# Hybrid decoder trunk on one core: a separate activation buffer at distance 0 for three uses, earlier transposes of the residual, and a later scaling of the final factors

## The chip, the cores and the metric

The kernel runs as one program on one core of a Trainium2 chip. The metric is the device time of one execution in microseconds; the time before is 628.7 us, the median of three runs (628.1 to 628.72). A profile of a further execution shows where the time of that execution went.

## What is computed

The input is one sequence of 256 tokens with 1024 features in float32. Layer 0 mixes tokens with a gated linear recurrence (8 heads), layer 1 with causal attention (8 heads; with 256 tokens only the own block counts). Each mixer is followed by a SwiGLU feed-forward part with 2816 hidden features, and a last RMSNorm closes the trunk.

```python
h = x
for layer in range(DEPTH):                      # DEPTH = 2
    y = rms_norm(h, norm_mix[layer])
    if layer % N_MIXERS == 0:
        y = hgrn2_mixer(y, hgrn_w_in[idx], hgrn_w_out[idx], lb_all[idx], hgrn_out_norm[idx])
    else:
        y = moba_mixer(y, moba_w_in[idx], moba_w_out[idx], rel_bias_table)
    h = h + y
    g, u = jnp.split(rms_norm(h, norm_ffn[layer]) @ ffn_w13[layer], 2, axis=-1)
    h = h + (silu(g) * u) @ ffn_w2[layer]
return rms_norm(h, final_norm)
```

## The kernel before

**Arithmetic.** Every product of activations with weights is made of three TensorE matmuls in float32r. A weight tile `raw` of 128 x 1024, brought by SyncE's queue, is rounded by ScalarE into `whi` (line 435), and VectorE writes the rest into `wlo` (line 437). An activation is split likewise into a pair with the names `xh`/`xl` (or `hh`/`hl` for the hidden features of the feed-forward parts). `mm_w` issues `whi*xh`, `wlo*xh`, `whi*xl` with the weights as the loaded operand and 256 tokens streaming; `mm_x` (used for the attention's values and for the second feed-forward part's way down) loads 128 tokens of the activation and streams 512 columns of weights. All of them are recorded under one line of the profile, L478 (the helper `mm`), so they are told apart by the names of their tiles and by their place in time.

**Order.** There is no automatic scheduler. The class `Order` holds a planner's clock: the main stream of weight matmuls is issued in the order of the code, and all other work (operations on ScalarE "A", VectorE "V", GpSimd "G", DMA issues "S", and small TensorE work "T") is queued with a due time and issued by `pump` when its inputs are planned to be ready; a "T" operation also waits until it has been ready for `early` ns of planned time (1500 unless it says otherwise). The order on each engine is therefore fixed when the program is built.

**Stages.** The opening and the recurrence's heads (to about 121 us in the trace), its way out (`out_rows` over `us`, to 149 us), feed-forward part 0 (`swiglu`, to 331 us: blocks of 48 matmuls on the way up and 24 on the way down, `down0`), the attention's values, queries and keys (to about 407 us), its way out (`out_rows` over `ao`, to 431 us), feed-forward part 1 (to 618 us: 48 matmuls of 256 tokens on the way up and 12 of 512 columns on the way down, `down1`), the final norm and the output. A part's first four blocks are computed together, over `k`, before the rest run block after block.

**Norms.** `residual` adds a way out to the residual `hT` (lines 632 to 636), splits the new `hT` into the next `xh`/`xl` (565, 567), and squares it (584, 585). `Stats.finish` then folds the sums (606), sums over partitions with two small matmuls (`ones`,`sqacc`), takes the root on GpSimd (617), and spreads it with two transposes (621) whose result ScalarE copies into `rrow` (624).

**Around the end.** The gain of the last norm is read by a DMA on ScalarE's queue into `bt` (1218) and scaled there by ScalarE (1219). `flip_h` transposes `hT` into the token-major `ht` in four groups of four 128 x 128 transposes (1228), each copied out by ScalarE (1231): groups 0 and 1 take the first 128 tokens, groups 2 and 3 the last 128. Only `Final`, at the very end, reads the gain and `ht`.

**Buffers.** `lay_out` places the tiles in a partition's memory. Call distance the start of an activation's buffer less the start of a weight buffer, modulo 256 bytes. Weight buffers take 4096 bytes, activation buffers 1024, and the gap of 48 floats (192 bytes) ahead of the `x` buffers puts all of these at distance 192. The rings `q1` and `k1`, which `hh0` and `hl0` reuse by `alias`, have gaps and widths of their own: their first buffer lies at distance 0, their second one at 192. `hh0`/`hl0` are taken in turn by hidden blocks 0, 7, 14 and 21; with the attention's values taking one turn between, distance 0 falls to blocks 0 and 14 of feed-forward part 0 and to blocks 7 and 21 of part 1. All other activation buffers lie at 192.

Of the kernel before, what the change touches and what calls it, by code (L numbers as in the profile page):

```python
# [15 lines left out]
P = 128  # L16
# [293 lines left out]
def ca(n, ptr=0):  # L310
    return n / 1.2 + 93 + 93 * ptr
# [14 lines left out]
def hybrid_trunk(ctx: ExitStack, tc: tile.TileContext, wts, xT, par, gfin, tab, onehot, masks, out):  # L326
# [10 lines left out]
    def ring(tag, shape, bufs, dt=FT):  # L337
        if tag not in rings:
            rings[tag] = Ring(lambda: sb.tile(shape, dt, name=tag, tag=tag, bufs=bufs), bufs)
        return rings[tag]  # L340
# [4 lines left out]
    def alias(tag, other, shape, dt=FT):  # L345

        o = rings[other]
        wide = [P, S + 48] if other in ("q1", "k1") else shape
        rings[tag] = Ring(lambda: sb.tile(wide, dt, name=tag, tag=other, bufs=o.bufs)[:, :shape[1]], o.bufs)
        rings[tag].past = o.past  # L350

    def lay_out():


        sb.tile([P, 96], FT, name="lead")
        for t in ("whi", "wlo"):
            ring(t, [P, SUB], NSUB, FR).make()
        sb.tile([P, 48], FT, name="gap")
        for k in range(KT):
            for part in "hl":  # L360
                ring(f"x{part}{k}", [P, S], 2, FR).make()
        for part in "qk":

            sb.tile([P, 16], FT, name=f"gap{part}1")
            rings[f"{part}1"] = Ring(lambda part=part: sb.tile([P, S + 48], FT, name=f"{part}1", tag=f"{part}1",
                                                              bufs=2)[:, :S], 2)
            rings[f"{part}1"].make()
            sb.tile([P, 16], FT, name=f"gap{part}2")
        for m in (2, 4, 8, 16, 32, 64):
            for part in "qk":  # L370
                ring(f"{part}{m}", [P, S], 2).make()

    def fixed(tag, shape, dt=FT):
        b = new(tag, shape, 1, dt)
# [6 lines left out]
    def bank(g, held=False):  # L381
        return rings["ps" + g].new(held)
# [97 lines left out]
    class X:  # L480
# [16 lines left out]
        def free(self):  # L497
            for b in (self.h, self.l):
                b.held = False
                b.readers.append(Mark(od.now))  # L500

    def mm_w(o, w, x, start=False, stop=False):
        mm(o, w.hi, x.hi, start=start)
# [299 lines left out]
    class Core:  # L803
# [162 lines left out]
        def result(self):  # L966
            h, so, b4 = self.h, self.so, self.b4
            due = 30
            us[h] = X("x", h)
            hi, lo = us[h].h, us[h].l  # L970
            u = new("u", [P, S], 3)
            od.op("V", 396, lambda: V.scalar_tensor_tensor(u.tile, b4[:, :S], gain(4)[:, h:h + 1], so.tile, op0=OP.mult,
                                                           op1=OP.mult), reads=[b4, so], alloc=[u], due=due)
            sto.add_half(h, lambda: b4[:, :S], [b4], due)
            od.op("A", ca(S), lambda: A.activation(hi.tile, u.tile, AF.Copy), reads=[u], alloc=[hi], due=due)
            od.op("V", cv(S), lambda: V.tensor_tensor(lo.tile, u.tile, hi.tile.bitcast(FT), op=OP.subtract),
                  reads=[u, hi], alloc=[lo], due=due)
# [51 lines left out]
    def swiglu(layer, x, stats, gu, down):  # L1029
# [3 lines left out]
        def hidden(j, b):  # L1033
            gs = new("sgq", [P, S], 3)
            sg = new("u", [P, S], 3)
            due = 6
            od.op("V", cv(S), lambda: V.tensor_tensor(gs.tile, b[:, :S], stats.row.tile, op=OP.mult),  # L1037
                  reads=[b, stats.row], alloc=[gs], due=due)
            od.op("A", ca(S), lambda: A.activation(sg.tile, gs.tile, AF.Sigmoid), reads=[gs], alloc=[sg], due=due)  # L1039
            od.op("V", cv(S), lambda: V.tensor_tensor(gs.tile, gs.tile, sg.tile, op=OP.mult), reads=[sg], writes=[gs], due=due)  # L1040
            od.op("V", cv(S), lambda: V.tensor_tensor(sg.tile, b[:, S:], gs.tile, op=OP.mult), reads=[b, gs], writes=[sg],
                  due=due)
            x = X("h", j % 7)
            hi, lo = x.h, x.l
            od.op("A", ca(S), lambda: A.activation(hi.tile, sg.tile, AF.Copy), reads=[sg], alloc=[hi], due=due + 6)
            od.op("V", cv(S), lambda: V.tensor_tensor(lo.tile, sg.tile, hi.tile.bitcast(FT), op=OP.subtract),
                  reads=[sg, hi], alloc=[lo], due=due + 6)
            hs[j] = x
# [83 lines left out]
    def attend(h, qb, kb):  # L1132
# [59 lines left out]
            mm(b3[:, :S], w[:, :P], pl.tile)  # L1192
            mm(b3[:, P:S], vv[:, 1, hs], pt(slice(0, P)), stop=True)
        od.op("T", ct(P) + 3 * MM, values, reads=[vv, vsplit[h], ptb, ph, pl], alloc=[b3], due=20)
        ao[h] = X("x", h)
        hi, lo = ao[h].h, ao[h].l
        od.op("A", ca(S), lambda: A.activation(hi.tile, b3[:, :S], AF.Copy), reads=[b3], alloc=[hi], due=22)
        od.op("V", cv(S), lambda: V.tensor_tensor(lo.tile, b3[:, :S], hi.tile.bitcast(FT), op=OP.subtract),
# [12 lines left out]
    for k in range(KT):  # L1211
# [4 lines left out]
    gf = new("bt", [P, NH * S])  # L1216
    gf.tile = bt.tile[:, :D]
    od.op("S", 60, lambda: A.dma_start(gf.tile, gfin.to_broadcast([P, D])), writes=[bt], nbytes=524288, due=60)
    od.op("A", ca(D), lambda: A.activation(gf.tile, gf.tile, AF.Copy, scale=-(float(D) ** 0.5) / 2), reads=[bt],
          writes=[gf], due=100)  # L1220
    ht = new("ii", [P, 2, D])

    def flip_h(tt, half):
        b = bank("B")

        def turn():
            for i in range(4):
                T.transpose(b[:, i * P:i * P + P], hT[:, 4 * half + i, tt * P:tt * P + P], ident)  # L1228
        od.op("T", 450, turn, reads=hb, alloc=[b], due=100)
        al = dict(alloc=[ht]) if (tt, half) == (0, 0) else dict(writes=[ht])  # L1230
        o = od.op("A", ca(512), lambda: A.activation(ht[:, tt, 512 * half:512 * half + 512], b[:, :], AF.Copy),
                  reads=[b], due=100 + tt + half, **al)
        if o.alloc == ():
            o.deps.append(ht.writers[0])

# [60 lines left out]
                      reads=[y], nbytes=262144, due=due)  # L1296

    def down1(k, hs, last=False):
        if not acc1:
            acc1[0] = [[main_bank("A") for _ in range(2)] for _ in range(2)]  # L1300
        ks = range(k, FTN if last else k + 1)
        keep["from"] = ws["sub"]
        w = {(kk, nh): piece("ffn_w2", 1, kk, 512 * nh, 512) for kk in ks for nh in range(2)}
        if last:
            od.op("A", 100, lambda: A.activation(warm, ones, AF.Sqrt), due=0)
        for tt in range(2):
            if not last:
                for nh in range(2):
                    mm_x(acc1[0][nh][tt][:, :], hs[k], w[k, nh], tt, start=(k == 0))
                continue  # L1310
            fin = Final(tt)
            for i, (nh, o, n) in enumerate(FIN):
                b = acc1[0][nh][tt]
                for kk in ks:
                    p = w[kk, nh]
                    mm_x(b[:, o:o + n], hs[kk], Piece(p.i, p.c + o, n), tt, stop=(kk == FTN - 1), cost=n / 2.4 + 2.5)
                wrote(b)
                fin.part(i)
            fin.end()
        keep["from"] = None  # L1320
        free_subs(ws["sub"])
        if not last:
            hs[k].free()
# [49 lines left out]
```

## Time and profile before

| | before |
|---|---|
| time, median of 3 runs | 628.7 us (628.1 to 628.72) |
| the profiled execution: time / span | 627.57 us / 625.8 us |
| TensorE clock granted in it | 0.998 |
| VectorE / ScalarE / GpSimd busy | 71% / 58% / 6% |
| DMA, read from HBM | 109.78 MB, 177 GB/s over the span |

The span is the time from the first to the last instruction that the profile holds; the profiled execution's own time is 1.8 us longer, and 1.1 us under the median. A matmul's end is modelled, so its row lasts longer than the step to the next one: the rate is read from the starts, or from the chain that ended last, whose rows give a start, a duration and a count of matmuls that follow each other.

### The profile page before, as it was taken

To read this page: it belongs to the slowest core of one execution; us is meant where nothing else is said; L and a number is where in the kernel's file an instruction comes from. 1 tells how busy PE (TensorE), PEld (TensorE's weight loads), DVE (VectorE), ACT (ScalarE), POOL (GpSimd) and SP (SyncE) were. 2 spreads that over 40 slices of the span, in tenths; PEclk is the share of its full clock that TensorE was granted. 3 is DMA by queue.
4 is the path that set the end of the run, shared out by engine and by line. 5 is a ranking of instruction groups with operands and counts; after the bars stand their busy time and mean duration, and the time that the engine had idled before them with its cause. 6 is when DMAs were issued, how large, how long until landed. Compare 5 with 4: busy or idle time off the path is not lost.

```text
span 625.8 us, 12443 instructions
## 1 busy us (share of the span) xinstructions
PE 615.6 (98%) x4848; PEld 592.8 (95%) x4848; DVE 443.1 (71%) x803; ACT 363.4 (58%) x715; POOL 36.7 (6%) x74
## 2 busy tenths in 40 slices
PE   8999999999999999999999999999999999999995
PEld 7899999999999999999998899999899999999994
DVE  6987989778686666666669678866676666666653
ACT  6779888857554444444447566565664444444443
POOL 0121112100300000000000000000100000000003
PEclk9999999999999999999999999999999999999999
DMA  8962534443996665666653665445645666556501
GB/s 315 331 208 93 179 103 169 132 139 106 236 282 197 201 187 193 195 198 191 189 198 121 215 206 169 139 162 172 202 160 178 203 202 200 184 182 181 163 2 67
DMA packets 31848, 111.83 MB, mean 179 GB/s; under 512 B 3804, under 2 KB 4221, under 8 KB 31789
## 3 DMA queue, kind: packets, MB, share of 16 engines
q1 hardware_dynamic: 30764, 108.71, 53.5%
q0 software_dynamic: 448, 1.25, 1.0%
q10 hardware_dynamic: 576, 1.08, 0.5%
q8 instruction: 38, 0.62, 0.4%
q14 instruction: 22, 0.17, 0.1%
HBM read 109.78 MB, written 1.25 MB: 177 GB/s over the span
## 4 chain that ended last, share of the span: by engine, by line
PE 79%; issue 16%; DVE 3%; DMA 1%; ACT 1%; POOL 1%; SPq 0%; ACTq 0%; DVEq 0%; POOLq 0%
PE psB L478 42%; PE psA L478 36%; DVE wlo L437 1%; DMA raw<-in_w_dram 1%; POOL ny L617 1%; DVE xl L567 0%; DVE yt L632 0%; DVE hT L634 0%; DVE sqacc L585 0%; PE psB L1228 0%; ACT whi L435 0%; PE psA L621 0%; DVE raw L1259 0%; ACT sq L1262 0%; ACT raw L1289 0%
## 5 line engine op out<-in xcount | busy, mean ns | idle before, releaser
L437 DVE TENSOR_TENSOR wlo<-raw,whi 128x1024 fp32r<-128x1024 f32 (+1 forms) x206 | 248.1, 1214 | 110.5 <-ACT whi L435 110.1
L435 ACT ACTIVATE whi<-raw 128x1024 fp32r<-128x1024 f32 (+1 forms) x205 | 213.0, 1050 | 149.0 <-issue 69.9
L478 PE MATMUL psA<-xh,whi 128*128 128x256 f32 x592 | 163.5, 279 | 0.0
L478 PE MATMUL psA<-xh,wlo 128*128 128x256 f32 x592 | 161.8, 277 | 0.0
L478 PE MATMUL psB<-xh,whi 128*128 128x256 f32 x560 | 157.9, 286 | 0.0
L478 PE MATMUL psA<-xl,whi 128*128 128x256 f32 x592 | 157.1, 277 | 0.0
L478 PE MATMUL psB<-xh,wlo 128*128 128x256 f32 x560 | 154.1, 279 | 0.0
L478 PE MATMUL psB<-xl,whi 128*128 128x256 f32 x560 | 149.9, 279 | 0.0
L478 PEld LDWEIGHTS psA<-xh,whi 128*128 128x128 f32 x592 | 111.2, 188 | 0.8 <-issue 0.5
L478 PEld LDWEIGHTS psA<-xh,wlo 128*128 128x128 f32 x592 | 111.3, 188 | 0.3
L478 PEld LDWEIGHTS psA<-xl,whi 128*128 128x128 f32 x592 | 108.2, 188 | 0.0
L478 PEld LDWEIGHTS psB<-xh,wlo 128*128 128x128 f32 x560 | 105.6, 189 | 0.7
L478 PEld LDWEIGHTS psB<-xh,whi 128*128 128x128 f32 x560 | 105.4, 188 | 0.8
L478 PEld LDWEIGHTS psB<-xl,whi 128*128 128x128 f32 x560 | 103.0, 189 | 0.0
L478 PE MATMUL psB<-hl,whi 128*128 128x256 f32 x176 | 48.7, 277 | 0.0
L478 PE MATMUL psB<-hh,whi 128*128 128x256 f32 x176 | 48.7, 277 | 0.0
L478 PE MATMUL psB<-hh,wlo 128*128 128x256 f32 x176 | 48.7, 276 | 0.0
L1039 ACT ACTIVATE u<-sgq 128x256 f32<-128x256 f32 x44 | 18.0, 410 | 38.9 <-DVE sgq L1037 38.7
L478 PE MATMUL psA<-wlo,hh 128*128 128x512 f32 x88 | 34.6, 393 | 0.0
L478 PE MATMUL psA<-whi,hl 128*128 128x512 f32 x88 | 34.5, 392 | 0.0
L478 PE MATMUL psA<-whi,hh 128*128 128x512 f32 x88 | 34.5, 392 | 0.0
L478 PEld LDWEIGHTS psB<-hl,whi 128*128 128x128 f32 x176 | 33.1, 188 | 0.0
(178 smaller groups left out, 789.6 us busy)
## 6 DMA issues: line engine op xcount, KB each, us to landing
raw<-in_w_dram SPq DMA_DIRECT2D x202, 512.0 KB, 4.2
raw<-in_w_dram SPq DMA_DIRECT2D x4, 256.0 KB, 5.0
bt<-scr POOLq DMA_DIRECT2D x8, 128.0 KB, 8.3
hT<-in_x_dram SPq DMA_DIRECT2D x1, 512.0 KB, 6.1
bt<-in_final_dram ACTq DMA_DIRECT2D x1, 512.0 KB, 4.9
out_dram<-raw ACTq DMA_DIRECT2D x2, 256.0 KB, 2.3
out_dram<-raw SPq DMA_DIRECT2D x2, 256.0 KB, 2.0
hT<-in_x_dram SPq DMA_DIRECT2D x2, 128.0 KB, 5.0
```

Source lines behind the costliest of these rows:

```text
L435: od.op("A", ca(n), lambda h=h, r=r, o=o, n=n: A.activation(h[:, :n], r[:, o:o + n], AF.Copy), reads=[r], alloc=[h], due=due)
L437: od.op("V", cv(n), lambda h=h, lo=lo, r=r, o=o, n=n: V.tensor_tensor(lo[:, :n], r[:, o:o + n], h[:, :n].bitcast(FT), op=OP.subtract), rea ...
L478: T.matmul(o, a, b, start=start, stop=stop, skip_group_check=True)
L617: od.op("G", 500, lambda: G.tensor_tensor(y.tile, v.tile, mhalf, op=OP.pow), reads=[v], alloc=[y], due=due)
L1039: od.op("A", ca(S), lambda: A.activation(sg.tile, gs.tile, AF.Sigmoid), reads=[gs], alloc=[sg], due=due)
```

## The change

Three things are edited.

1. `q1` and `k1` become ordinary rings, so all their buffers, and with them `hh0`/`hl0`, lie at distance 192. Behind all rings a gap of 16 floats and one pair `zh`/`zl` is laid out, at distance 0. `across()` hands it out, and it is used for head 0 on the recurrence's way out (`us[0]`), for block 0 of feed-forward part 0, and for head 0 on the attention's way out (`ao[0]`). What is laid out behind the rings moves up by 1088 bytes, 64 bytes modulo 256 and modulo 1024.
2. The transposes of `hT` get a due time of 24 in place of 100, `early` times of 7000, 8500, 10000 and 11500 ns, and PSUM banks of group A in place of B.
3. The scaling of the final gain is issued in `down1` at block 2, in place of ahead of feed-forward part 1.

```diff
-        for part in "qk":
-            sb.tile([P, 16], FT, name=f"gap{part}1")
-            rings[f"{part}1"] = Ring(lambda part=part: sb.tile([P, S + 48], FT, name=f"{part}1", tag=f"{part}1",
-                                                              bufs=2)[:, :S], 2)
-            rings[f"{part}1"].make()
-            sb.tile([P, 16], FT, name=f"gap{part}2")
-        for m in (2, 4, 8, 16, 32, 64):
+        for m in (1, 2, 4, 8, 16, 32, 64):
             for part in "qk":
                 ring(f"{part}{m}", [P, S], 2).make()
+        sb.tile([P, 16], FT, name="gap2")
+        for part in "hl":
+            ring(f"z{part}", [P, S], 1, FR).make()
...
+    def across():
+        return X("z", "", 1)
...
-            us[h] = X("x", h)
+            us[h] = X("x", h) if h else across()
...
-            x = X("h", j % 7)
+            x = across() if (layer, j) == (0, 0) else X("h", j % 7)
...
-        ao[h] = X("x", h)
+        ao[h] = X("x", h) if h else across()
...
-    od.op("A", ca(D), lambda: A.activation(gf.tile, gf.tile, AF.Copy, scale=-(float(D) ** 0.5) / 2), reads=[bt],
-          writes=[gf], due=100)
...
-        b = bank("B")
+        b = bank("A")
...
-        od.op("T", 450, turn, reads=hb, alloc=[b], due=100)
+        od.op("T", 450, turn, reads=hb, alloc=[b], due=24, early=7000.0 + 1500.0 * (2 * tt + half))
...
     def down1(k, hs, last=False):
+        if k == 2:
+            od.op("A", ca(D), lambda: A.activation(gf.tile, gf.tile, AF.Copy, scale=-(float(D) ** 0.5) / 2), reads=[bt],
+                  writes=[gf])
```

How the order moves is seen at three places; the number in a name is that of the buffer in the built program, and the lines of the changed kernel are 473 for 478, 430 for 435 and 1226 for 1228.

TensorE, in the first four blocks of feed-forward part 1, at the spread of the norm's factor (`ident,ny`), before:

```order
L478 MATMUL psB<-xh_6022,whi 128x256
L478 MATMUL psB<-xh_6022,wlo 128x256
L478 MATMUL psB<-xl_6041,whi 128x256 x4
L621 MATMUL psA<-ident,ny 128x128 x2
L478 MATMUL psB<-xl_6041,whi 128x256 x4
L478 MATMUL psB<-xh_6069,whi 128x256
```

And after:

```order
L473 MATMUL psB<-xh_6021,wlo 128x256
L473 MATMUL psB<-xl_6040,whi 128x256 x2
L1226 MATMUL psA<-ident,hT 128x128 x4
L621 MATMUL psA<-ident,ny 128x128 x2
L473 MATMUL psB<-xl_6040,whi 128x256 x6
L473 MATMUL psB<-xh_6067,whi 128x256
L473 MATMUL psB<-xh_6067,wlo 128x256
L1226 MATMUL psA<-ident,hT 128x128 x4
```

The first group of transposes stands right ahead of the spread, the second eight matmuls behind it, the third ten matmuls on.

TensorE, at the first block on the way down in feed-forward part 1, where two of the four groups stood before:

```order
L478 MATMUL psB<-xl_6041,whi 128x256
L1228 MATMUL psB<-ident,hT 128x128 x4
L478 MATMUL psB<-xh_6069,whi 128x256
L478 MATMUL psB<-xh_6069,wlo 128x256
L478 MATMUL psB<-xl_6079,whi 128x256
L1228 MATMUL psB<-ident,hT 128x128 x4
```

After, none is left there; the fourth group stands earlier, behind the first step of the fifth block on the way up:

```order
L473 MATMUL psB<-xh_5989,wlo 128x256
L473 MATMUL psB<-xl_6009,whi 128x256
L1226 MATMUL psA<-ident,hT 128x128 x4
L473 MATMUL psB<-xh_5999,whi 128x256
L473 MATMUL psB<-xh_5999,wlo 128x256
```

So all four groups come before the first block on the way down, where two stood inside it or behind it.

ScalarE, around the last norm ahead of feed-forward part 1, before:

```order
L565 ACTIVATE xh_6022<-hT,pv 128x256
L1218 DMA bt<-in_final_dram 128x1024
L584 ACTIVATE sq<-hT 128x512
L1219 ACTIVATE bt<-bt 128x1024
L565 ACTIVATE xh_6069<-hT,pv 128x256
L565 ACTIVATE xh_6071<-hT,pv 128x256
```

And after:

```order
L565 ACTIVATE xh_6021<-hT,pv 128x256
L1218 DMA bt<-in_final_dram 128x1024
L584 ACTIVATE sq<-hT 128x512
L565 ACTIVATE xh_6067<-hT,pv 128x256
L565 ACTIVATE xh_6069<-hT,pv 128x256
```

The scaling of the gain is no longer between the squares of the first half of `hT` and the splits of the second half; it stands some 30 rows later, among the blocks of feed-forward part 1.

More of the change, by code (lines that the diff above doesn't have):

```diff
@@ L347, in alias @@
         o = rings[other]
-        wide = [P, S + 48] if other in ("q1", "k1") else shape
-        rings[tag] = Ring(lambda: sb.tile(wide, dt, name=tag, tag=other, bufs=o.bufs)[:, :shape[1]], o.bufs)
+        rings[tag] = Ring(lambda: sb.tile(shape, dt, name=tag, tag=other, bufs=o.bufs), o.bufs)
         rings[tag].past = o.past
@@ L1228, in turn @@
                 T.transpose(b[:, i * P:i * P + P], hT[:, 4 * half + i, tt * P:tt * P + P], ident)
-        od.op("T", 450, turn, reads=hb, alloc=[b], due=100)
+        od.op("T", 450, turn, reads=hb, alloc=[b], due=24, early=7000.0 + 1500.0 * (2 * tt + half))
         al = dict(alloc=[ht]) if (tt, half) == (0, 0) else dict(writes=[ht])
         o = od.op("A", ca(512), lambda: A.activation(ht[:, tt, 512 * half:512 * half + 512], b[:, :], AF.Copy),
-                  reads=[b], due=100 + tt + half, **al)
+                  reads=[b], due=24 + tt + half, **al)
         if o.alloc == ():
```

## The prediction

> **What bounds the kernel now.** I read the page first: busy times, then the chain that ended last.
>
> ```profile
> PE 615.6 (98%) x4848; PEld 592.8 (95%) x4848; DVE 443.1 (71%) x803; ACT 363.4 (58%) x715; POOL 36.7 (6%) x74
> ...
> PE 79%; issue 16%; DVE 3%; DMA 1%; ACT 1%; POOL 1%; SPq 0%; ACTq 0%; DVEq 0%; POOLq 0%
> ```
>
> TensorE is the bound nearly everywhere, so only two things can move the time: how fast its matmuls follow each other, and where it stands still. The chain, in order of time, shows the first (start, duration, what, count):
>
> ```profile
> 164.89 0.22 PE psB L621 x2
> 165.11 13.39 PE psA L478 x118
> 178.50 2.86 PE psB L478 x24
> ...
> 186.82 2.72 PE psB L478 x24
> ...
> 292.90 2.86 PE psB L478 x24
> ...
> 515.16 5.47 PE psB L478 x48
> 520.62 2.73 PE psA L478 x12
> 523.36 5.65 PE psB L478 x48
> 529.01 2.77 PE psA L478 x12
> ...
> 599.14 5.65 PE psB L478 x48
> ```
>
> Matmuls of 256 tokens come at two rates. The good one is 2.72/24 = 113.3 ns a step. The bad one is 5.65/48 = 117.7 ns; it begins at 523.4 and is still there at 599.1. It begins right behind the block at 520.62, which is hidden block 7 of feed-forward part 1, one of the four that use the buffer at distance 0; the other two in sight, at 178.50 and 292.90, are blocks 0 and 14 of part 0, where each step takes 2.86/24 = 119.2 ns. There the good rate follows. So distance 0 costs some 6 ns a step where the activation streams, and where it is the loaded operand (part 1) a lasting bad rate follows. Is it the clock? The two stretches side by side (engines' busy time, then clock, DMA share, GB/s):
>
> ```profile
> 466.30:515.00 48.70, 48.70 (x358) 45.75 (x357) 31.12 (x42) 22.70 (x31) 0.00 (x0) 1.00 0.60 189
> 523.40:604.60 81.20, 81.20 (x588) 76.58 (x587) 51.16 (x66) 36.63 (x48) 0.00 (x0) 1.00 0.51 159
> ```
>
> The granted clock is 1.00 in both and DMA is lighter in the slow one, so it is neither. The rate is a state of TensorE's stream which, once taken, lasts until something breaks the stream.
>
> Where TensorE stands still, its timeline at the norm ahead of feed-forward part 1 shows (start, duration, last the idle time and what ended it):
>
> ```profile
> 438.71 0.62 PE L478 MATMUL psB<-xl,whi 128*128 128x256 f32 x4
> 440.14 0.58 PE L478 MATMUL psA<-ones,sqacc 128*128 128x1 f32 x4 [0.81 <-DVE sqacc L606]
> ...
> 443.01 0.63 PE L478 MATMUL psB<-xl,whi 128*128 128x256 f32 x4
> 444.07 0.43 PE L621 MATMUL psA<-ident,ny 128*128 128x128 f32 x2 [0.42 <-POOL ny L617]
> ```
>
> Four steps from 438.71 end at 439.16, and the sums start at 440.14: 0.98 us lost. Four slow steps from 443.01 end at 443.48, and the spread starts at 444.07: 0.59 us lost.
>
> **Part 1 of the change: the gain's scaling moves.** Who is late at 440.14? The other engines' timelines (idle time last):
>
> ```profile
> 433.36 1.28 DVE L636 TENSOR_TENSOR hT<-psA,hT 128x512 f32<-128x512 f32 x2
> 435.03 1.06 ACT L1219 ACTIVATE bt<-bt 128x1024 f32<-128x1024 f32 x1 [2.39 <-DMA bt<-in_final_dram]
> 436.00 0.89 ACT L565 ACTIVATE xh<-hT,pv 128x256 fp32r<-128x256 f32 x2
> 436.52 0.89 DVE L567 SCALAR_TENSOR_TENSOR xl<-hT,pv,xh 128x256 fp32r<-128x256 f32 x2 [1.88 <-ACT xh L565]
> 439.57 0.42 DVE L606 TENSOR_TENSOR sqacc<-sqacc 128x256 f32<-128x256 f32 x1
> 439.91 2.36 DVE L437 TENSOR_TENSOR wlo<-raw,whi 128x1024 fp32r<-128x1024 f32 x2
> 442.18 0.15 DVE L614 TENSOR_SCALAR nv<-psA 128x2 f32<-128x2 f32 x1
> 442.41 1.60 POOL L617 TENSOR_TENSOR ny<-nv,mhalf 128x2 f32<-128x2 f32 x1 [97.87 <-DVE nv L614]
> ```
>
> The second half's `hT` begins to be there at 434.04 (433.36 + 0.68), but ScalarE sits behind the scaling, which waits 2.39 us for its DMA, and splits only at 436.00; VectorE stands 1.88 us for it. With the scaling gone this chain starts 1.88 us sooner, the limit being `hT` itself. The folded sums end at 439.99 - 1.88 = 438.11, ahead of 439.16: **-0.98**. Next late: `nv` on VectorE, behind two weight remainders of 2.36 us, at about 440.5, and the root, 1.60 us, ends near 442.2. TensorE reaches the spread at 443.48 - 0.98 = 442.50, and after the change the first four transposes stand ahead of it as well: **-0.59**, with some 0.3 us to spare even without these. The scaling (1.06 us) goes to block 2, where ScalarE is busy 22.70 of 48.70 us; the wait for the DMA is long over. At nothing; without that cover it would cost its 1.06 us.
>
> **Part 2: the transposes move.** Their number is the same. In the place that they leave, and at the spreads, the chain reads:
>
> ```profile
> 142.32 0.22 PE psA L621 x2
> 142.54 6.71 PE psB L478 x57
> ...
> 460.73 0.44 PE psB L1228 x4
> 461.17 1.06 PE psB L478 x9
> ...
> 465.79 0.44 PE psB L1228 x4
> 466.23 5.12 PE psB L478 x45
> ```
>
> A group takes 0.44 us and brings one longer step behind it, before as after: 0, with bounds of 0.15 us to either side for rates in the short stretches between. Their copies go ahead on ScalarE (a group of 0.60 us each, below) of the factor's copy and of weight roundings:
>
> ```profile
> 444.54 0.39 ACT L624 ACTIVATE rrow<-psA 128x256 f32<-128x256 f32 x1 [2.96 <-PE psA L621]
> L1231 ACT ACTIVATE ii<-psB 128x512 f32<-128x512 f32 x4 | 2.4, 599 | 1.6 <-PE psB L1228 1.6
> ```
>
> ScalarE stood idle for 2.96 us just there, so 2.4 us fit. But each group also breaks the stream, and these rows show that the rate behind a break is either: 6.71/57 = 117.7 and 1.06/9 = 117.8 against 5.12/45 = 113.8 and, behind the spread at 164.89, 13.39/118 = 113.5. Of the groups in this excerpt, the one at 460.73 reads the first 128 tokens and leaves the bad rate, the last one reads the other 128 and leaves the good one. The two differ by 512 bytes in where `hT` lies against the stream's buffer, 160 and 672 bytes modulo 1024; after the change it is 96 and 608. The last group is again of the second kind, and I take it to leave the good rate. This decides much, since behind it no break comes until the end.
>
> **Part 3: the buffers.** Block 7 of part 1 is no longer at distance 0, so nothing turns the rate at 520. The blocks at 515.16 and 523.36 differ by 0.18, the ways down behind them by 0.04 at most; ten of the one (523.36 to 599.14 at 8.42 us a round) and nine of the other: 1.8 + 9 x 0.02 = **-2.0**. Block 14 of part 0 falls from 2.86 to 2.72: **-0.14**. Block 0 was at distance 0 and stays so. `ao[0]` newly pays **+0.14**. `us[0]` pays between 0 and 0.14, as its stretch is cut up by the heads' own matmuls and partly slow already: **+0.1**.
>
> The tiles behind the rings move by 64 bytes, so breaks ahead of 178 us may fall the other way. Known ones: the spread at 164.89 now leaves 118 steps at 113.5; at 117.7 they would cost 0.5, until the block at distance 0 behind it. Others, like 57 steps behind 142.54, could win 0.25. Bounds -0.5 to +0.8; I take **+0.3**, by the spread at 142.32: its factor's tile lies 448 bytes modulo 1024 from the stream's buffer, as that at 164.89 will (512 now), and it leaves the bad rate.
>
> **Sum.** -0.98 - 0.59 - 2.0 - 0.14 + 0.14 + 0.1 + 0.3 = -3.2 us, against the profiled execution's 627.6: 624.4. The median of the runs shown is 1.1 us above that execution, so the forecast is 628.7 - 3.2 = **625.5 us**.
>
> [...]
>
> **Rivals.**
> *The last group of transposes leaves the bad rate.* For: two of the four stretches quoted behind a break are slow, 608 has no row. Against: the row at 465.79. Price: the 2.0 isn't won, and the 67 us up to 523, now good, turn bad (the fourth group stands some 30 steps ahead of the place that the first one leaves at 459.9, so at about 456) at 0.2 us a round of 8.2: +1.6. 628.7 - 3.2 + 2.0 + 1.6 = 629.1.
> *Feed-forward part 0 stays slow* (slower than before). If the spread at 164.89 leaves the bad rate, and block 0 at distance 0, entered from the bad rate, doesn't restore the good one, 150 us from 181 to 331 run at 117.7: 72 steps a round of 8.16 us, 18.4 rounds, 4.4 ns each: +5.8. Both must happen. For: the spread at 142.32. Against: both rows at distance 0 are followed by the good rate; yet both are entered from it. 625.5 + 0.2 (the rest of the 0.5) + 5.8 = 631.5.
> *The stalls don't close*, the sums being held by something that the scaling hides: 625.5 + 1.6 = 627.1. Against: VectorE's row with 1.88 names ScalarE alone.
> *The buffer does nothing*: the rate at 523 turns for another reason, by the time in the stream, and turns again: 625.5 + 2.0 = 627.5. Against: rounds at 515.16 and before are alike, and it turns in the very block at distance 0.
>
> **How the numbers follow.** Chances: forecast 0.62, last group 0.16, part 0 slow 0.07, stalls stay 0.09, buffer without effect 0.06. The forecast's own spread, from the bounds of parts 2 and 3 (-0.8 and +0.5 about the value taken, 0.15 for the transposes, 0.1 for `us[0]`) and 0.1 for the measurement, is 624.3 to 626.4. The range reaches up to the last group's 629.1, and leaves out part 0 and the tails: 624.3 to 629.3. 0.2% is 1.26 us, about what a measurement of this kernel can tell from no change, so faster is below 627.4: nearly all of 0.62, 0.07 of the stalls' case and 0.03 of the buffer's, less tails: 0.71. Slower, over 630.0: 0.08. Between: 0.21.
>
> **What would show it.** In the profile after: the sums and the spread in feed-forward part 1 without idle time ahead of them; ScalarE's splits within 0.2 us of `hT`; rounds of 8.2 us from the last transposes to the end; block 14 of part 0 at 2.72; `ao[0]`'s 24 steps near 119 ns. A round of 8.4 us behind the fourth group would prove me wrong on the rate, steps of 117.7 between 181 and 331 would show the dear case, and idle time at the sums that names another engine the third.

## The result and the profile after

The changed kernel takes 623.98 us, the median of four runs (623.45 to 624.26), against 628.4 us for the kernel before on the same chip (627.93 to 628.72): a ratio of 0.9933 [0.992, 0.9947]. The direction of the forecast was right. Its size was not: 623.98 lies 1.5 us under the 625.5 us forecast and 0.3 us under the low end of the range. The profiled execution took 623.94 us, with a span of 622.2 us. One execution of the kernel before, of 682.65 us at a granted clock of 0.849, is left out of every comparison below.

The page of the changed kernel, first TensorE's busy time and share, then the shares of the chain that ended last:

```profile
PE 613.2 (99%) x4848; PEld 591.3 (95%) x4848; DVE 443.0 (71%) x803; ACT 363.6 (58%) x715; POOL 36.7 (6%) x74
...
PE 96%; DMA 2%; DVE 1%; ACT 1%; issue 0%; SPq 0%; ACTq 0%; DVEq 0%
```

Before, 79% of the chain lay on TensorE and 16% was put down to "issue", since the chain left TensorE at the spread and followed GpSimd's empty queue backwards. Now nearly all of it lies on TensorE, and it no longer leaves TensorE at the spread.

The chain of the changed kernel in order of time (start, duration, what, count), at the places that the prediction spoke of:

```profile
143.04 6.49 PE psB L473 x57
...
165.09 13.40 PE psA L473 x118
178.49 2.86 PE psB L473 x24
...
292.89 2.72 PE psB L473 x24
...
446.07 9.88 PE psB L473 x87
455.95 0.44 PE psA L1226 x4
456.39 5.13 PE psB L473 x45
...
519.02 2.75 PE psA L473 x12
521.76 5.47 PE psB L473 x48
...
595.68 5.47 PE psB L473 x48
```

From the last group of transposes at 455.95 to the end, every block takes 5.47 us; the bad 5.65 us of before is gone, and block 7 (519.02) takes 2.75 us as its neighbours do. Block 14 of feed-forward part 0 (292.89) takes 2.72 us for 2.86. The 118 steps behind the spread at 164.87, for which I feared the bad rate, take 13.40/118 = 113.6 ns; the 57 steps at 143.04, slow before, take 6.49/57 = 113.9.

The other engines' timelines at the norm ahead of feed-forward part 1 (start, duration, engine, line, operation, and last the idle time with what ended it):

```profile
433.49 1.28 DVE L636 TENSOR_TENSOR hT<-psA,hT 128x512 f32<-128x512 f32 x2
434.21 0.91 ACT L565 ACTIVATE xh<-hT,pv 128x256 fp32r<-128x256 f32 x2 [1.44 <-DVE hT L636]
437.80 0.43 DVE L606 TENSOR_TENSOR sqacc<-sqacc 128x256 f32<-128x256 f32 x1
439.30 0.50 PE L473 MATMUL psA<-ones,sqacc 128*128 128x1 f32 x4
440.41 0.15 DVE L614 TENSOR_SCALAR nv<-psA 128x2 f32<-128x2 f32 x1
440.64 1.60 POOL L617 TENSOR_TENSOR ny<-nv,mhalf 128x2 f32<-128x2 f32 x1 [96.28 <-DVE nv L614]
442.25 0.60 PE L1226 MATMUL psA<-ident,hT 128*128 128x128 f32 x4
442.68 0.38 PE L621 MATMUL psA<-ident,ny 128*128 128x128 f32 x2
```

ScalarE splits at 434.21, right behind the first of the two additions (433.49 + 0.68 = 434.17, one addition taking 0.68 us), and its wait now names `hT`. The folded sums end at 438.23, ahead of TensorE's 439.30; the root ends at 442.24, and TensorE passes through the first group of transposes to the spread at 442.68. No idle time stands in either of TensorE's rows.

Stage by stage, each worked out from the start of the first weight matmul of a stage to that of the next stage's first, in the two profiled executions (times of the profile before):

| stage | before | after | difference | forecast |
|---|---|---|---|---|
| opening, from 5.0 us to 22.8 | 17.86 | 18.20 | +0.34 | 0 |
| recurrence's heads, to 121.5 | 98.65 | 98.89 | +0.24 | with the next row |
| way out of the recurrence and part 0's first four blocks, to 178.3 | 56.85 | 56.28 | -0.57 | +0.4 |
| part 0 from block 0, to 331.0 | 152.64 | 152.48 | -0.16 | -0.14 |
| attention's heads and its way out, to 431.5 | 100.48 | 100.78 | +0.30 | +0.14 |
| part 1's norm, transposes and first way down, to 469.8 | 38.37 | 36.63 | -1.74 | -1.57 |
| part 1, to 523.2 | 53.37 | 53.39 | +0.01 | 0 |
| part 1, behind block 7, and the tail | 102.59 | 100.56 | -2.03 | -2.0 |

The sum is -3.61 us, and the two profiled executions differ by 627.57 - 623.94 = 3.63 us. By medians the gain is larger, 628.4 - 623.98 = 4.4 us. Two things were to be explained: the terms that differ from the forecast, and the difference between medians and profiles.

### The profile page after: what moved, and what is told of

Same layout as the page of the kernel before. It is cut to its first block, busy times and chain, and to the rows that moved or that the text cites. A ratio compares the mean times of both kernels' runs of the same rounds, so it can differ in the third digit from the quotient of the medians.

```text
span 622.2 us, 12444 instructions
## 1 busy us (share of the span) xinstructions
PE 613.2 (99%) x4848; PEld 591.3 (95%) x4848; DVE 443.0 (71%) x803; ACT 363.6 (58%) x715; POOL 36.7 (6%) x74
## 4 chain that ended last, share of the span: by engine, by line
PE 96%; DMA 2%; DVE 1%; ACT 1%; issue 0%; SPq 0%; ACTq 0%; DVEq 0%
PE psA L473 50%; PE psB L473 45%; DMA hT<-in_x_dram 1%; DMA raw<-in_w_dram 1%; PE psB L1180 0%; PE psA L1226 0%; DVE wlo L432 0%; ACT sq L584 0%; ACT xh L565 0%; PE psA L621 0%; DVE raw L1257 0%; ACT sq L1260 0%; ACT raw L1287 0%; DVE sqacc L585 0%; PE psB L621 0%
## 5 line engine op out<-in xcount | busy, mean ns | idle before, releaser
L473 PE MATMUL psA<-xh,whi 128*128 128x256 f32 x584 | 161.0, 279 | 0.0
L473 PE MATMUL psA<-xh,wlo 128*128 128x256 f32 x584 | 159.5, 276 | 0.0
L473 PE MATMUL psA<-xl,whi 128*128 128x256 f32 x584 | 154.9, 277 | 0.0
L473 PE MATMUL psB<-xh,whi 128*128 128x256 f32 x552 | 154.7, 284 | 0.0
L473 PE MATMUL psB<-xh,wlo 128*128 128x256 f32 x552 | 151.2, 278 | 0.0
L473 PE MATMUL psB<-xl,whi 128*128 128x256 f32 x552 | 146.9, 278 | 0.0
L473 PE MATMUL psB<-hl,whi 128*128 128x256 f32 x168 | 46.4, 276 | 0.0
L473 PE MATMUL psB<-hh,whi 128*128 128x256 f32 x168 | 46.4, 276 | 0.0
L473 PE MATMUL psB<-hh,wlo 128*128 128x256 f32 x168 | 46.4, 276 | 0.0
L473 PEld LDWEIGHTS psB<-hh,whi 128*128 128x128 f32 x168 | 31.5, 188 | 0.0
```

The source lines that it names most:

```text
L473: T.matmul(o, a, b, start=start, stop=stop, skip_group_check=True)
```

## The experiments

Twelve more runs were made, each with a profile: one of the kernel before, two of the changed kernel, and nine of eight variants. The first took the kernel before once more, unchanged, to see what the 1.1 us between its median and its profiled execution are.

> The kernel before, unchanged, profiled a second time. Open is why its first profiled execution (627.57 us) lies 0.8 us under the median of its runs, while that of the changed kernel lies on its median. Theory: other executions of it run some stretch at the other of the two rates of matmuls (113.3 or 117.7 ns a step), so this profile, if it comes out near 628.4 us, shows some 0.8 us more in one named stretch, about 180 steps at the bad rate. Rival: the excess is spread evenly or lies outside the span; then all stretches agree with the first profile within 0.1 us and only the span or what is around it grows.

Measured: 628.37 us (627.9 to 630.27, ten executions); every stage behind the opening agrees with the first profile within 0.02 us, except the stage with the stall at the sums, 9.21 for 9.12 us. The opening takes 18.66 for 17.86 us. So this execution, at the median, has no stretch at the other rate: it has a longer opening and a slightly longer stall. That doesn't explain the median, though: over all 14 traces of this document the opening takes 17.28 to 18.66 us, so that the first profile's 17.86 is an ordinary one and this 18.66 the longest. The theory of a stretch at another rate doesn't hold for this execution; that others have none isn't shown, and the run with the transposes alone, below, has one.

**One part alone: the scaling of the gain** (the transposes and the buffers as before).

```diff
-    od.op("A", ca(D), lambda: A.activation(gf.tile, gf.tile, AF.Copy, ...), reads=[bt], writes=[gf], due=100)
...
     def down1(k, hs, last=False):
+        if k == 2:
+            od.op("A", ca(D), lambda: A.activation(gf.tile, gf.tile, AF.Copy, ...), reads=[bt], writes=[gf])
```

> Only the scaling of the final gain is moved; buffers and transposes are those of before. Theory: both stalls at the norm ahead of feed-forward part 1 go, 0.98 + 0.59 us, and nothing else changes: 1.6 us off the span, between the way out of the attention and the first block on the way down; the bad rate from 523 us on stays. Rival: without the transposes ahead of the spread the second stall stays in part: between 1.0 and 1.6 us.

Measured: 626.62 us (626.26 to 626.9, seven executions), a ratio of 0.997 [0.9959, 0.9981]. Its chain at the two places:

```profile
435.99 3.64 PE psB L478 x32
439.62 0.34 PE psA L478 x4
439.96 2.94 PE psB L478 x24
442.89 0.22 PE psA L621 x2
443.11 16.02 PE psB L478 x136
```

The sums (439.62) and the spread (442.89) follow the matmuls ahead of them without a gap: both stalls are gone, without any transposes ahead of the spread. But the 136 steps behind the spread take 16.02 us, where the kernel before has 15.44: behind the break stands the bad rate now, and it takes back 0.58 us. Summed over the norm and the first way down, the profile's gain is 1.1 us, and by the medians it is 1.7. The executions lie within 0.64 us of each other; those of the kernel before lie between 627.25 and 630.27 us over all chips. That the wait on the gain's DMA makes the difference in spread is likely, and not shown: the ten executions with the transposes alone, which wait for it as well, lie within 1.15 us.

**One part alone: the buffers** (the first edit of the change, its part of the diff above down to `ao[h]`; scaling and transposes as before).

> Only the buffers are changed (the rings q1 and k1 plain, the separate pair at distance 0 for three uses); the scaling and the transposes are those of before. Theory: the bad rate behind block 7 of feed-forward part 1 doesn't begin, 2.0 us; block 14 of part 0 wins 0.16; the first head of the attention's way out costs 0.3; the heads of the recurrence, whose tiles have moved, come out within 0.5 us of before: 1.9 us off the span in sum. Rival: the last group of transposes, which in this order stands behind the first block on the way down, leaves the bad rate, and the rounds stay at 8.4 us: 0 to 1.6 us longer than before.

Measured: 629.49 us (626.17 to 631.2, ten executions), a ratio of 1.0001 [0.998, 1.0021]. The buffers alone win nothing in the median. The chain, from the wait on the gain to block 7:

```profile
429.26 5.57 DMA bt<-in_final_dram
...
440.54 4.46 PE psB L473 x24
...
466.53 0.44 PE psB L1228 x4
466.97 5.30 PE psB L473 x45
...
517.14 5.65 PE psB L473 x48
```

Two things are to be seen. The last group of transposes, at 466.53, here leaves the bad rate (5.30/45 = 117.8 ns, where before had 113.8), and it lasts from there on (5.65 us for 48 steps at 517.14, 4.48 us for 38 at 525.56), through blocks that have nothing at distance 0: this is the first rival of the prediction, and it took back what the buffer won. And 24 steps at 440.54 take 4.46 us, 186 ns each. The windows of this kernel, the stretch from 440.90 and one behind it, say what that is (from and to, the stretch, the busy times, then granted clock, DMA share, GB/s); the last row is the same place in the kernel before:

```profile
440.90:444.30 3.40, 3.40 (x19) 3.40 (x19) 2.38 (x4) 0.50 (x1) 1.60 (x1) 0.53 0.62 182
445.00:449.00 4.00, 4.00 (x37) 4.00 (x36) 2.36 (x2) 2.83 (x4) 0.00 (x0) 1.00 0.54 197
...
440.50:444.00 3.50, 3.15 (x26) 2.94 (x26) 2.97 (x4) 1.07 (x2) 1.59 (x1) 1.00 0.58 160
```

And its timeline, ScalarE's wait and TensorE's (idle time last):

```profile
434.86 1.06 ACT L1219 ACTIVATE bt<-bt 128x1024 f32<-128x1024 f32 x1 [3.07 <-DMA bt<-in_final_dram]
439.96 0.58 PE L473 MATMUL psA<-ones,sqacc 128*128 128x1 f32 x4 [1.48 <-DVE sqacc L606]
```

Here ScalarE waited 3.07 us for the gain (2.39 before), TensorE stood idle for 1.48 us (0.81 in the same row of before), and just behind that its granted clock fell to 0.53 for 3.4 us. The stage in which that lies took 12.84 us for 11.94: another 0.9 us, although the stall at the spread is gone there. The ten executions lie in two clumps, four between 626.17 and 626.5 us and six from 629.44 on; the profile belongs to the upper one. The lower clump is 2 us under the kernel before's 628.35 us on that chip, what the forecast gave this part. No profile of it exists, so whether the good rate, the clock or both make it stays open.

**Block 7 back at distance 0**, all else as after.

```diff
-            x = across() if (layer, j) == (0, 0) else X("h", j % 7)
+            x = across() if (layer, j) in ((0, 0), (1, 7)) else X("h", j % 7)
```

> The changed kernel, with the separate pair at distance 0 used a fourth time, for hidden block 7 of feed-forward part 1. Theory: that block, the loaded operand at distance 0, turns the rate from 113.3 to 117.7 ns a step, and it stays so to the end: rounds of 8.4 in place of 8.2 us from about 521 us on, 2.0 us longer than the changed kernel, nothing else changed. Rival: the rate of before turned at that place for another reason (the time in the stream, or the double rings); then the rounds stay at 8.2 us and the time is that of the changed kernel within 0.1 us.

Measured: 625.71 us (625.4 to 626.17), a ratio of 0.9959 [0.9944, 0.9974]. Its chain:

```profile
513.73 5.47 PE psB L473 x48
519.20 2.73 PE psA L473 x12
521.93 5.65 PE psB L473 x48
...
597.71 5.66 PE psB L473 x48
```

The rate turns in block 7 and stays bad to the end: the 612 weight matmuls from there on take 86.95 us for 84.88. That is +2.07 us for the -2.0 of the prediction, and every other stage behind the opening is as after.

**After once more, the halves swapped, and block 0 and the two others at 192.** These three ran on one chip. In the second, groups 0 and 1 take the last 128 tokens and groups 2 and 3 the first:

```diff
+        s = 1 - tt
...
-                T.transpose(b[:, i * P:i * P + P], hT[:, 4 * half + i, tt * P:tt * P + P], ident)
+                T.transpose(b[:, i * P:i * P + P], hT[:, 4 * half + i, s * P:s * P + P], ident)
...
-        o = od.op("A", ca(512), lambda: A.activation(ht[:, tt, 512 * half:512 * half + 512], b[:, :], AF.Copy),
+        o = od.op("A", ca(512), lambda: A.activation(ht[:, s, 512 * half:512 * half + 512], b[:, :], AF.Copy),
```

> The changed kernel, unchanged, profiled a second time. Theory: it has left few breaks behind which the rate can fall either way, so its executions agree: span within 0.4 us of 622.2, and every stretch within 0.1 us of the first profile. Rival: its rates differ from execution to execution, and one stretch differs by 0.3 us or more.

Measured: 623.57 us (623.25 to 624.23), a ratio of 0.9923 [0.9907, 0.9939]; each stage as in the first profile within 0.04 us, except the opening, 17.77 for 18.20 us.

> The changed kernel with the two halves of the tokens swapped in the groups of transposes: groups 0 and 1 take the last 128 tokens, groups 2 and 3 the first, so that the group behind which no break comes any more reads the 512 bytes that the prediction takes to leave the bad rate. Theory (where hT lies against the stream's buffer, modulo 1024 bytes, decides: 96 bad, 608 good): the rounds behind the fourth group, from about 456 us on, are 8.4 in place of 8.2 us to the end, 3.7 us longer than the changed kernel. Rival: the rate behind a break is set by something else; the rounds stay at 8.2 us and the time is that of the changed kernel.

Measured: 623.82 us (623.44 to 624.46), a ratio of 0.9927 [0.9911, 0.9942]. Its chain behind the third and the fourth group:

```profile
445.60 9.88 PE psB L473 x87
...
455.91 5.13 PE psB L473 x45
```

The same 9.88 and 5.13 us as after, although the address that each group reads against the stream's buffer is that of the other half. So the bytes modulo 1024, by which the prediction chose the good rate for the last group, do not decide it, for these two breaks.

For the third, the gap ahead of the separate pair grows by 192 bytes, so that it lies at distance 192, and what follows stays where it is after the change:

```diff
-        sb.tile([P, 16], FT, name="gap2")
+        sb.tile([P, 64], FT, name="gap2")
...
+        sb.tile([P, 208], FT, name="fill")
```

> The changed kernel with the separate pair at distance 192 in place of 0; a filler keeps all other addresses modulo 1024 bytes. Theory: distance 0 costs where it is used and restores nothing here, since all the stretches ahead of it are at the good rate already: block 0 of feed-forward part 0 wins 0.16, the attention's first head 0.3, the recurrence's first head 0 to 0.2: 0.5 to 0.7 us shorter than the changed kernel. Rival: distance 0 is what leaves the good rate behind it; then the stretch behind one of the three uses runs at 117.7 ns a step, up to 5.8 us longer in feed-forward part 0.

Measured: 623.36 us (623.03 to 623.42), a ratio of 0.9917 [0.9899, 0.9935]. Its chain at block 0 of part 0 and at the last group of transposes:

```profile
178.09 2.72 PE psB L474 x24
...
455.60 5.30 PE psB L474 x45
```

Block 0 takes 2.72 for 2.86 us, and the `ao` matmuls 10.66 for 10.83. The last group leaves the bad rate here (5.30 us for 45 steps), yet it holds only to the first block on the way down: from 463.7 on the good one stands. With the buffers alone it had passed through the blocks on the way down (2.77 us each at 514.37 and 522.79, and still 5.65 us for 48 steps between them). Part 0 runs at the good rate with nothing at distance 0 ahead of it, so block 0 restores nothing there. The profiled span, 621.6 us for 622.2 after, fits both: by an estimate from 5.65 and 5.47 us a block, the bad rate in the 17 blocks behind 463.7 would have added 3.1 us, and in part 0 some 5.8 us by the prediction's estimate. Whether distance 0 would restore the good rate from the bad one was not put to the test, since no run entered block 0 at the bad rate.

**The tiles behind the rings back at their old place modulo 1024** (960 bytes more ahead of them), all else as after:

```diff
+        sb.tile([P, 240], FT, name="fill")
```

> The changed kernel with a filler of 960 bytes behind the separate pair, so that what is laid out behind the rings (identity, hT, the factors, the masks, the attention's tiles) lies as before modulo 1024 bytes. Theory: the 64 bytes by which these had moved set the rates behind the breaks of the recurrence; so the 57 steps behind the spread at 142 us, good after the change, are bad again (+0.25 us), and those to 153 us with them (+0.15), while the heads from 56 to 62 us and 103 to 121 us go back as well; the groups of transposes leave the same rates as after the change. In sum within 0.5 us of the changed kernel. Rival: the rates of the recurrence were set by q1 and k1 at distance 192 or by us[0] at 0, and stay as after the change.

Measured: 623.71 us (623.41 to 624.06), a ratio of 0.9924 [0.9908, 0.994]. Its chain at the spreads:

```profile
142.16 6.71 PE psB L474 x57
...
164.72 13.39 PE psA L474 x118
```

The 57 steps are at 6.71 us again, as before the change. The twelve runs and the two first profiles give 14 traces: in the six with the old addresses these 57 steps take 6.71 or 6.72 us, in the eight with the new ones 6.49. So the 64 bytes do set this stretch. From the 240th to the 672nd weight matmul, among the recurrence's heads, 75.25 us pass here and 75.51 after; the next two stages, to 149 and to 167 us, take 27.55 and 18.36 us here, 27.32 and 18.08 after. So the move by 64 bytes is worth +0.26 - 0.23 - 0.28 = -0.25 us, where the prediction had +0.3. And `us[0]` at distance 0, which this kernel has and the kernel before has not, costs nothing: 27.55 for 27.61 us.

**The wait made longer.** The kernel before, with a second read of the gain into a part of `bt` that nothing uses then, ahead of the gain's own:

```diff
+    od.op("S", 60, lambda: A.dma_start(bt.tile[:, D:], gfin.to_broadcast([P, D])), writes=[bt], due=59.9)
```

> Before with a second read of the gain (512 KB more, into a half of a buffer that nothing uses then) ahead of the gain's own DMA, so that the scaling and with it the sums wait longer; TensorE's order is that of before. Theory (TensorE waits for the scaling, and a longer wait also halves the clock for some 3.4 us, as in the run with the buffers alone): the stall at the sums grows by about 1 us or more from 0.98 us, behind it some 16 steps take about 214 ns, 3120-3188 takes 10 us or more for 9.12 us, 3188-3284 about 12.8 us for 11.94 us, and the median lies 1.5 to 3 us above before. Rival (only the wait counts, the clock was chance): the steps behind it stay at 113 to 120 ns, and the median rises by the wait alone. Second rival (the gain doesn't set the wait): 3120-3188 stays within 0.1 us of 9.12 us.

Measured: 632.08 us (630.79 to 633.72, four executions, of which the profiled one was the longest), a ratio of 1.0056 [1.0037, 1.0075]. Two pieces of its chain:

```profile
430.69 7.93 DMA bt<-in_final_dram
...
444.72 5.21 PE psB L478 x24
```

Its windows, from the end of the wait to behind the spread:

```profile
443.70:447.20 3.50, 3.46 (x16) 3.49 (x17) 3.37 (x4) 1.47 (x2) 1.19 (x1) 0.50 0.39 129
447.20:449.90 2.70, 2.70 (x16) 2.70 (x15) 0.00 (x0) 0.00 (x0) 0.41 (x1) 0.55 0.89 267
450.00:454.00 4.00, 4.00 (x37) 4.00 (x36) 2.36 (x2) 2.79 (x4) 0.00 (x0) 1.00 0.29 109
```

And its timeline at the sums (idle time last):

```profile
443.74 0.98 PE L478 MATMUL psA<-ones,sqacc 128*128 128x1 f32 x4 [4.20 <-DVE sqacc L606]
```

TensorE stands still for 4.20 us, and the clock is 0.50 to 0.55 for the next 6.2 us: 24 steps in 5.21 us, 217 ns each. That is nearly twice as long as in the run with the buffers alone, and more steps than the 16 that I expected. The stage with the stall takes 12.91 us (9.12 before), the next 13.89 (11.94). Both parts of the theory came out, TensorE's wait for the scaling and about half the clock behind it, and the price of the longer wait was more than expected: 3.8 us more in the stage with the wait (its idle time grew by 3.39) and 1.95 us more in the next in this execution, the longest of the four; the median rose by 3.7. The clock fell inside the stall here: from 438.60 to 443.70 it is 0.91.

**One part alone: the transposes** (scaling and buffers as before):

```diff
-        b = bank("B")
+        b = bank("A")
...
-        od.op("T", 450, turn, reads=hb, alloc=[b], due=100)
+        od.op("T", 450, turn, reads=hb, alloc=[b], due=24, early=7000.0 + 1500.0 * (2 * tt + half))
...
-                  reads=[b], due=100 + tt + half, **al)
+                  reads=[b], due=24 + tt + half, **al)
```

The due time of ScalarE's copies moves with that of the transposes, here as in the whole change.

> Before with the placing of the residual transposes alone changed: they go out in blocks 0 to 3 of part 1's way up, and the gain is scaled where before scales it and the buffers stay. Theory (sum of parts): the stall at the sums stays (3120-3188 about 9.1 us for 9.12 us), the stall at the spread (0.59 us) is kept or filled in part by the first group, the bad rate behind block 7 is gone if a group now ends it (523 to the end 84.9 us for 86.94 us): median about 626.0 us, 2.0 to 2.6 us under before. Rival (the transposes need the other two edits to be free): a group waits for a bank or for the scaling, 3188-3408 longer than 29.3 us, and the median lies within 1 us of before.

Measured: 628.25 us (627.8 to 628.95, ten executions), a ratio of 0.9996 [0.9986, 1.0005]: no difference. Its chain:

```profile
443.31 1.61 POOL ny L617
...
515.81 5.47 PE psB L478 x48
521.28 2.73 PE psA L478 x12
524.01 5.66 PE psB L478 x48
```

My expectation was wrong where it gave the -2.0 to this part. The groups end at 458, some sixty us ahead of block 7, and no break comes behind block 7; so it turns the rate as before (5.47 at 515.81, 5.66 at 524.01). The way out of the first block gains 1.84 us, the stages ahead of it lose 0.22, 1.14 and 0.46: the 1.76 us of transposes are carried from one place to another, nothing more. The root still comes late, and TensorE still waits for it at the spread.

One more thing is to be seen in it: up to 440 us TensorE's order and all addresses are those of the kernel before, yet behind the three small transposes at 415.68 the steps run at 117.8 ns here, and at 113.3 ns in both profiles of the kernel before. The attention's last small matmuls, at 419.19, hand the bad rate on to the 105 steps behind them, and it lasts to the stall; from 414.31 to 432.13 it costs 0.57 us. The rate behind that break isn't settled by order and addresses alone.

**The version without distance 0 against the changed kernel**, both once more, on one chip.

> The changed kernel with the separate buffer at distance 192 in place of 0, a second time, beside the changed kernel itself on the same chip. Theory (distance 0 costs time where its three uses stand and its rate is given back by none of them): 672 to 864 about 27.1 us for 27.3 us, block 0 of part 0 2.72 us for 2.86 us, the ao matmuls 10.66 us for 10.83 us, the fourth group's leaving 10.43 us for 10.25 us; median 0.2 to 0.5 us under the changed kernel's in the same job. Rival (the opening decides): the medians lie within 0.15 us.

> The changed kernel unchanged, on the same chip as the version without distance 0. Theory: 623.25 to 624.3 us as in its earlier runs, every stage behind the opening within 0.05 us of the first profile, and 0.2 to 0.5 us above the version without distance 0. Rival: the opening's spread (17.3 to 18.7 us) covers that difference, and the medians lie within 0.15 us.

Measured: 623.25 us (622.9 to 623.57, five executions) without distance 0, 623.71 us (623.32 to 624.32, six) for the changed kernel; ratios to before 0.9914 [0.9901, 0.9926] and 0.9923 [0.991, 0.9935]. The medians differ by 0.46 us, as expected; the stages account for less. Block 0 (-0.14), the `ao` matmuls (-0.17) and the last group's leaving (+0.18) come out as the first time, but the stage with `us[0]` takes 27.32 us, as after, and not 27.11: in the first profile 57 steps between 129 and 136 us had the good rate, in this one they have not. The last 24 of them, in the first profile and in this one:

```profile
133.45 2.74 PE psB L474 x24
...
133.22 2.83 PE psB L474 x24
```

The two profiles are of one and the same kernel, so order and addresses don't settle the rate here either. Behind the opening the two profiles of this job differ by 0.2 us. So the version without distance 0 has the lowest medians of all that ran, by 0.21 us under the changed kernel on the first chip and 0.46 on the second, with intervals that overlap; less than half of the 0.46 is in a stage that I could name.

## Why the prediction was wrong in size, and right in direction

**The bound and the two rates.** Right. That distance 0 turns the rate in block 7, and that the turn lasts to the end, is shown from both sides: the 612 weight matmuls from there on take 2.06 us less after the change, and 2.07 us more with block 7 put back and all else equal. The rival by which the buffer does nothing has fallen. That a rate lasts until something breaks the stream was said too firmly: without distance 0 the bad rate (5.30 us for 45 steps) ended at the first block on the way down, at 463.7, behind which no group of transposes stands.

**The stalls.** Right: -1.74 for -1.57, the order of waits was as forecast (the fold 438.23 for 438.11, the root 442.24 for 442.2), and the run with the scaling alone shows that the scaling's place, and not the transposes, closes both.

**The transposes.** Right at 0 when alone. But that the last group leaves the good rate was a guess on a wrong reason: the halves swapped leave the same rates. It came true in the changed kernel and in its repeats; in the run with the buffers alone, with the group at its old place, it did not, and the bad rate from there on took back the 2 us in the profiled execution; without distance 0 the group left the bad rate too, for 45 steps. That it left the good one here was luck, and what decides it stays open. The chance of 0.16 for that rival was no overestimate.

**Block 14 and `ao[0]`.** -0.14 forecast, 2.72 for 2.86 measured; +0.14 forecast, +0.17 by the run without distance 0. Of this only some 0.1 is in the steps of `ao[0]`, at 120 ns; the rest is in the 18 steps of the next head, which run at 118 ns behind it, so distance 0 under the streaming operand wasn't always followed by the good rate. With the tiles back at their old place these 18 are at 113 ns again. Part 0 didn't turn slow, and block 0 had no part in that.

**First step that failed: "+0.3" for the 64 bytes and "+0.1" for `us[0]`.** In the two rows of the table between 22.8 and 178.3 us they came to +0.24 - 0.57 = -0.33 us instead of +0.4. The run with the tiles back puts the 64 bytes at -0.25 and `us[0]` at 0 or a little below. The bounds that the prediction had given for the 64 bytes (-0.5 to +0.8) held; the value taken from the spread at 142.32 did not, because the stretch behind 164.87 kept its rate and the one behind 142.82 gained. This is 0.7 us of the error, some half of it covered by the opening, which was 0.34 us longer than in the profile before.

**Second step that failed: "The median of the runs shown is 1.1 us above that execution, so the forecast is 628.7 - 3.2".** That carries the 1.1 us over to the changed kernel as if every execution had them, without a reason. The likeliest source is a wait that the change removes: from the issue of the gain's DMA to the scaling 4.92 and 5.01 us pass in the two profiles of the kernel before, 5.37 with the transposes alone and 5.60 with the buffers alone. The kernels that still wait for the gain run from 627.25 to 630.27 us (before) and from 630.79 to 633.72 us (the wait made longer); with the scaling moved alone the spread is 0.64 us, and 14 executions of the changed kernel lie between 623.25 and 624.32 us. So the changed kernel's profiled execution, 623.94 us, is at its median, while that of the kernel before was under its own (628.35 us and more in the later jobs). From the base of the profiled execution, the forecast would have been 624.4 us, within 0.5 us of what was measured. But where the 1.1 us lie isn't shown: the second profile of the kernel before, at the median, has only 0.09 us in the stall and 0.8 in an uncommonly long opening, and the run with the transposes alone, which still waits, spreads over 1.15 us. A stretch at the other rate, 0.57 us in that run, is a third source that isn't excluded.

**The parts don't add up.** By medians alone, the scaling gives -1.7 us, the buffers nothing that the interval tells from zero, the transposes nothing; together they give 4.4 us. In the profiles, the buffers' part was worth 2 us where the last break ahead left the good rate (5.47 us a block behind block 7 after the change), and not where it left the bad one (5.65 us at 517.14 with the buffers alone).

## What to carry to other kernels

Where matmuls stream without a break, look for the last thing that breaks the stream ahead of a long stretch: here a rate of 113.3 or 117.8 ns is taken there and was kept for up to 150 us (the good one from 181.35 to 330.97 us of the changed kernel), and a part that only changes the rate wins nothing if that break hands on the bad one. The difference between a median and one profiled execution shouldn't be carried over to a changed kernel unless it is known what makes it; here a forecast from the profiled execution came within 0.5 us, and one from the median missed by 1.5. Moving small work off an engine that heads a chain (a scaling of 1.06 us that waits 2.39 us for a DMA) is worth what the chain waits, here 1.57 us, less what the rate behind the next break takes back (0.58 us with the scaling alone); where the wait was longer, a lower clock came on top: 0.53 for 3.4 us with the buffers alone, 0.50 to 0.55 for 6.2 us with the second read of the gain.

## What the runs showed of the hardware

A short stand of TensorE was followed by a lower clock in two executions and so cost more than itself. At the same place, by the idle time in TensorE's row of the sums, 0.81 us left the clock at 1.00 (kernel before), 1.48 us was followed by 3.4 us at 0.53 (buffers alone), 4.20 us by 6.2 us at 0.50 to 0.55 (longer wait). Behind the 4.20 us 24 steps of 256 tokens took 217 ns each. Each is one execution; that the idle time is what lowers the clock is likely by them, and what decides between 0.81 and 1.48 us isn't shown.

The rate behind a break of the stream isn't a matter of chance at every place, nor fixed at every place: 57 steps near 143 us followed the addresses in all 14 traces (6.71 or 6.72 us in six, 6.49 in eight), while the steps behind 415.68 us in the attention's way out (113.3 ns in both profiles of the kernel before, 117.8 with the transposes alone), and 57 steps between 129 and 136 us in two profiles of one kernel (2.74 and 2.83 us for the last 24 of them), had two rates under the same order and the same addresses. What decides there stays open.
